# A hybrid attention block on one core: stick-breaking summed by parts, eight more gates by 7-product units, two branches moved beside the forgetting heads

## The chip, the cores and the metric

The kernel runs on one core of one Trainium2 chip. The metric is the time of the whole program on the device in microseconds (us), as the median of several runs; a profiled execution gives the trace. The engines that matter are TensorE (PE, with its weight loads as PEld), VectorE (DVE), ScalarE (ACT), GpSimd (POOL) and SyncE (SP); the last two mostly issue DMAs.

## What is computed

One decoder block over 1024 tokens of width 1024, in float32. The normalized input is projected into queries, keys and values of two kinds of attention with 8 heads of 64 each, queries of a memory attention with 4 heads of 128 over 256 memory tokens, 8 forget logits, and three gates of width 1024.

```python
z = einsum(q, k) * HD ** -0.5                       # stick-breaking, strictly causal
log_rem = where(strict, log_sigmoid(-z), 0.0)
after = cumsum(log_rem, reverse=True) - log_rem
w = where(strict, exp(log_sigmoid(z) + after), 0.0) # o_sb = w @ v
...
z = einsum(q, k) * HD ** -0.5 + F[t] - F[s]         # forgetting, F = cumsum(log f)
p = softmax(where(causal, z, NEG_INF))              # o_fox = p @ v
...
gates = sigmoid(gate_logit)
merged = gates[0] * (o_sb @ w_sb) + gates[1] * (o_fox @ w_fox) + gates[2] * (o_mem @ w_mem)
x = x + merged @ w_out
x = x + relu(rmsnorm(x) @ w_up) ** 2 @ w_down
```

## The kernel before

**Numbers.** A float32 operand is split into a high and a low part (`split`, L1027): ScalarE copies the high part, VectorE subtracts. A product takes three passes on TensorE (high-high, high-low, low-high). A matmul's free size is at most 512 columns, one PSUM bank.

**Order.** A planner written in Python (`Machine`, L186) runs generator processes at build time and emits the instructions of each engine in the order in which its own cost estimates let them begin. A process yields an `Op` on an engine, a `Get` of a buffer from a list of places, a `Sleep`, or an event. `spawn(gen, late)` gives a process a priority: the smaller the number, the earlier it is served among those that wait. Operations with `side=True` run only when no other operation of that engine is ready; all projections and branches are of this kind, so they fill what the attention heads leave of TensorE. Each engine executes its emitted list in order, and waits on semaphores for what it needs.

**Stages.**
1. Norms of the tokens and their transposes (`prologue`), then values of the forgetting heads, gates 8 and 9 and the memory's keys and values.
2. Six *units* (`unit_products`, L1365), the projections `sbk, sbq, mq, fxk, fxq, sbv` of 512 output columns each, by a scheme of 7 block products in place of 8 (`KINDS`). Sums of weight blocks are made by `unit_prep`, results of the 7 products are added up by `unit_evict` (L1439) and brought into their final form by `unit_final` (L1468), through 10 buffers `SN`. Results go to DRAM scratch. `PP`, `SC` and `PV` banks are lent to the units and given back in the last one: two each.
3. Attention (`second_part`, `load_pairs`, `units`): 4 pairs of stick-breaking heads, then 4 pairs of forgetting heads; each pair has 8 units of two query tiles of 128. A tile's scores are made in chunks of 512 columns in one of two `SC` banks.
   - `sb_tile` (L786): ScalarE makes 1 - beta (`rho`) and beta of a chunk; VectorE masks the diagonal, scans `rho` from the right into running products, and multiplies beta by them.
   - `fox_tile` (L824): VectorE masks the diagonal, finds each chunk's maximum and its negative; ScalarE exponentiates with that and sums; then the two chunks' maxima are merged and ScalarE scales the whole tile by factor over sum.
   - `unit` (L875): the weights are transposed on TensorE, split by ScalarE and VectorE, multiplied with the values' high and low halves (which stand side by side in 128 columns); ScalarE and VectorE add both halves of the output, and SP stores it.
   - `memory` (L559): 4 heads by 2 halves, each in `mem_attention`; starts once the last stick-breaking pair is over, so it runs beside the forgetting heads. It uses `RR` tiles (three, shared with `sb_tile`) and `HT` tiles (head operands; 12 + 7 + 4).
   - Filler for TensorE: the 22 other gates (`dense_gate`, `dense_T`), 2 halves of 8 blocks by 3 passes each. Gates 16 to 23 get their sigmoid at eviction, the others are stored as they are and get it when they are used.
4. When all gates are done the normalized input is freed (`all_h`, event `closed`) and `O` tiles open in its place. Then three branches follow, memory (`dense_branch(0)`), stick-breaking (`dense_branch(1)`), forgetting (`last_branch`). `operands` (L1563) and `bring` (L1550) fetch head outputs from DRAM into `RAW` tiles and split them. A branch multiplies with the gate on VectorE from `PP` banks, of which there are four once the heads are over (`more_banks`).
5. The output projection, the norm, and the MLP, by 7-product schemes.

Loads of head operands, values, memory and gate weights are issued from GpSimd's queue, which is in order; outputs, gates and branch operands go through SP's.

Of the kernel before, what the change touches and what calls it, by code (L numbers as in the profile page):

```python
# [21 lines left out]
P = 128  # L22
# [21 lines left out]
def tile_hybrid_block(  # L44
# [40 lines left out]
    C = Pool("c", st=32, st16=8, ss=4)  # L85
# [10 lines left out]
    def mmbank():  # L96
# [6 lines left out]
    above = C.p.tile([P, P + 1], F32, tag="above", name="above")  # L103
    nc.gpsimd.memset(above, 0.0)
    nc.gpsimd.affine_select(out=above, in_=above, pattern=[[-1, P + 1]], compare_op=ALU.is_ge,
                            fill=NEG, base=0, channel_multiplier=1)
    tri, strict = above[:, :P], above[:, 1:]
# [10 lines left out]
    o_scr = [dram.tile([512, S], F32, name=f"o_scr{b}", tag=f"o_scr{b}") for b in range(3)]  # L118
    gate_scr = dram.tile([3 * D, S], F32, name="gate_scr", tag="gate_scr")
# [4 lines left out]
    v_scr = {k: dram.tile([P, ST * 512], F32, name=f"v_{k}", tag=f"v_{k}") for k in ("sb0", "sb1", "fx0", "fx1")}  # L124
    m_scr = [dram.tile([P, 4, 512], F32, name=f"m_scr{c}", tag=f"m_scr{c}") for c in range(2)]
# [5 lines left out]
    def stat(n, dt=F32):  # L131
        return (C.t("st", [P, 8], dt) if n <= 8 else C.t("st16", [P, 16], dt))[:, :n]
# [204 lines left out]
    ES, OO, EL, RR, HT, PH, PL, OB, VV, BK = (Places([]) for _ in range(10))  # L337
# [127 lines left out]
    def small_loads():  # L465
# [9 lines left out]
        def scale():  # L475
            nc.vector.tensor_scalar(gq2, gq2, HD ** -0.5, None, ALU.mult)
            nc.vector.tensor_scalar(gmq, gmq, P ** -0.5, None, ALU.mult)
# [81 lines left out]
    def memory():  # L559
        yield pairs[3].over  # L560
# [33 lines left out]

    def mem_attention(h, half, kv, q):
# [8 lines left out]
        def scores_of(t2):  # L604
# [9 lines left out]
            def maxima():  # L614
                nc.vector.tensor_reduce(mx, sc.rearrange("p (t m) -> p t m", m=MEM), AX.X, ALU.max)
                nc.vector.tensor_scalar(mx, mx, -1.0, None, ALU.mult)
# [7 lines left out]
            yield Op("DVE", dve_time(512) + SMALL, maxima)  # L624
# [161 lines left out]
    def sb_tile(pair, b, i, beta):  # L786
# [4 lines left out]
        def chunk(ci, c, m, u):  # L791
# [6 lines left out]
            def sigmoids():  # L798
                nc.scalar.activation(rho[:, c:c + u], sc[:, :u], AF.Sigmoid, scale=-HD ** -0.5)  # L799
                nc.scalar.activation(beta[:, c:c + u], sc[:, :u], AF.Sigmoid, scale=HD ** -0.5)  # L800

            yield Op("PE", mm_time(m, m), scores)
            if c + u == n:
                dg = sc[:, u - P:u]
                yield Op("DVE", 0.22, lambda: nc.vector.tensor_tensor(dg, dg, strict, ALU.add))
# [6 lines left out]
        def scan():  # L812
            rev = rho[:, n - 1::-1] if n == D else rho[:, 0:n][:, ::-1]
            nc.vector.tensor_tensor_scan(out=rev, data0=rev, data1=zero.to_broadcast([P, n]),  # L814
                                         initial=1.0, op0=ALU.mult, op1=ALU.add)

        def weights():
            nc.vector.tensor_tensor(beta[:, 0:n - 1], beta[:, 0:n - 1], rho[:, 1:n], ALU.mult)

        yield Op("DVE", 0.1 + 0.00215 * n, scan, 0.14)  # L820
        yield Op("DVE", dve_time(n), weights)
        RR.put(rho)

    def fox_tile(pair, b, i, e):  # L824
# [5 lines left out]
        st = stat(16)  # L830
        mx, nx, l, f, t_, m = (st[:, c0:c0 + 2] for c0 in range(0, 12, 2))

        def chunk(ci, c, cols, u):
# [6 lines left out]
            def maxima():  # L840
                if c + u == n:
                    dg = sc[:, u - P:u]
                    nc.vector.tensor_tensor(dg, dg, tri, ALU.add)
                nc.vector.tensor_reduce(mx[:, ci:ci + 1], sc[:, :u], AX.X, ALU.max)  # L844
                nc.vector.tensor_scalar(nx[:, ci:ci + 1], mx[:, ci:ci + 1], -1.0, None, ALU.mult)
            yield Op("PE", mm_time(cols, cols), scores)
            yield Op("DVE", (0.22 if c + u == n else 0.0) + dve_time(u) + SMALL, maxima)
# [653 lines left out]
    def second_part():  # L1501
# [11 lines left out]
        for ev in proj_over:  # L1513
            yield ev
# [1064 lines left out]
```

## Time and profile before

| | |
|---|---|
| median of 3 runs | 1707.92 us (1707.22 to 1709.28) |
| profiled execution | 1706.93 us |
| its span, first to last instruction | 1705.1 us |
| matmuls | 9186 |
| VectorE busy | 1346.3 us (79%) |
| ScalarE busy | 886.8 us (52%) |
| bytes moved by DMA | 271.72 MB |

How to read the rows: `L1119 PE MATMUL pp<-hi,whi` is an instruction of line 1119 on TensorE that writes tile `pp` and reads `hi` and `whi`; then come shapes, a count, and, after a bar, busy microseconds and mean nanoseconds of one, and, after another, the idle time of that engine just before them and whom it waited for. In the view of one line, three numbers with slashes are the least, median and greatest duration in ns, and two times are the first and last start. Tables by stretch give busy microseconds of each engine with the number of instructions. In a row of waits, the numbers are microseconds in total, how often, and the longest. A DMA row ends with KB of one transfer and the median us from issue to landing.

### The profile page before, as it was taken

The numbers are of one execution on the slowest core, as the hardware profiler recorded it, in microseconds if no ns is written. First come the engines' busy times: TensorE is split into PE (matmuls) and PEld (weight loads), VectorE is DVE, ScalarE is ACT, GpSimd is POOL, SyncE is SP. The second block draws the span as 40 slices with busy tenths as digits, with TensorE's granted clock in tenths as the row PEclk, the third lists the DMA queues.
The fourth block names the chain that finished last, engine by engine and source line by source line (L and its number), as shares of the span: only waits on it lengthen the run. The fifth ranks groups of instructions, "written<-read, shape, count | busy, mean of one in ns | idle before, by whom it ended". The sixth has DMA issues, their size and how long they took to land.

```text
span 1705.1 us, 25350 instructions
## 1 busy us (share of the span) xinstructions
PE 1691.7 (99%) x9186; PEld 1442.8 (85%) x9186; DVE 1346.3 (79%) x2321; ACT 886.8 (52%) x1635; POOL 256.0 (15%) x441
## 2 busy tenths in 40 slices
PE   9999999999999999999999999999999999999998
PEld 9998899998888888888888887878888887888887
DVE  7977678868999888888656898987777776788775
ACT  6445555556676798889733446533233344332331
POOL 0000000043322233241000011021211120000000
PEclk9999999999999999999999999999999999999999
DMA  7545444576544453553375642144444484554532
GB/s 242 162 144 191 135 124 149 157 245 187 160 128 123 113 176 112 183 164 110 100 238 168 217 179 94 56 162 141 156 153 149 142 289 180 195 206 148 198 123 74
DMA packets 131406, 271.72 MB, mean 159 GB/s; under 512 B 15761, under 2 KB 43409, under 8 KB 131281
## 3 DMA queue, kind: packets, MB, share of 16 engines
q1 hardware_dynamic: 99600, 169.94, 29.2%
q0 software_dynamic: 31680, 100.17, 19.5%
q8 instruction: 72, 1.18, 0.3%
q14 instruction: 54, 0.43, 0.1%
HBM read 181.44 MB, written 88.60 MB: 158 GB/s over the span
## 4 chain that ended last, share of the span: by engine, by line
PE 83%; issue 7%; DVE 5%; DMA 2%; POOL 2%; ACT 1%; SPq 0%; POOLq 0%; DVEq 0%; ACTq 0%
PE pp L1119 21%; PE pp L2518 7%; PE pp L1405 7%; PE pp L1848 6%; PE sc L1405 5%; PE tr L904 4%; PE tr L2518 4%; PE sc L2518 4%; PE sc L1119 3%; PE sc L1848 3%; PE pv L2518 2%; PE pv L921 2%; PE pp L921 2%; PE pv L1405 2%; POOL s_scr L1865 2%
## 5 line engine op out<-in xcount | busy, mean ns | idle before, releaser
L1119 PE MATMUL pp<-hi,whi 128*128 128x512 f32 x368 | 147.6, 401 | 0.0
L1119 PE MATMUL pp<-hi,wlo 128*128 128x512 f32 x368 | 145.0, 394 | 0.0
L1119 PE MATMUL pp<-lo,whi 128*128 128x512 f32 x368 | 144.8, 393 | 0.0
L1030 DVE TENSOR_TENSOR wlo<-raw,whi 128x1024 fp32r<-128x1024 f32 (+1 forms) x82 | 100.0, 1221 | 38.9 <-ACT whi L1029 38.6
L2518 PE MATMUL pp<-h,sop 128*128 128x512 f32 x540 | 128.7, 395 | 1.4 <-DVE sop L1784 1.4
L2518 PEld LDWEIGHTS pp<-h,sop 128*128 128x128 f32 x540 | 101.1, 187 | 26.5 <-DVE sop L1784 1.8
L1848 PE MATMUL pp<-h,oh 128*128 128x512 f32 x384 | 120.9, 396 | 0.7 <-ACT cu L1934 0.6
L1029 ACT ACTIVATE whi<-raw 128x1024 fp32r<-128x1024 f32 (+1 forms) x82 | 86.8, 1059 | 52.4 <-PE pp L1405 18.7
L911 DVE TENSOR_TENSOR ptl<-tr,pth 128x512 fp32r<-128x512 f32 (+1 forms) x160 | 98.8, 627 | 11.0 <-ACT pth L909 10.6
L909 ACT ACTIVATE pth<-tr 128x512 fp32r<-128x512 f32 (+1 forms) x160 | 86.7, 558 | 28.5 <-PE tr L904 15.5
L814 DVE TENSOR_TENSOR_SCAN r<-r,sm 128x896 f32<-128x896 f32 (+4 forms) x64 | 85.5, 1345 | 3.5 <-ACT r L799 3.4
L2436 ACT ACTIVATE h<-t 128x2048 fp32r<-128x2048 f32 x16 | 30.7, 1919 | 110.4 <-DVE t L1784 97.9
L1848 PEld LDWEIGHTS pp<-h,oh 128*128 128x128 f32 x384 | 71.7, 187 | 19.2 <-ACT cu L1934 1.5
L1119 PEld LDWEIGHTS pp<-hi,wlo 128*128 128x128 f32 x368 | 69.1, 188 | 16.4
L1119 PEld LDWEIGHTS pp<-lo,whi 128*128 128x128 f32 x368 | 69.5, 189 | 10.3
L1119 PEld LDWEIGHTS pp<-hi,whi 128*128 128x128 f32 x368 | 69.4, 189 | 10.1
L1848 PE MATMUL pp<-h,ol 128*128 128x512 f32 x192 | 75.9, 396 | 0.0
L1841 ACT ACTIVATE oh<-raw 128x512 fp32r<-128x512 f32 x64 | 39.4, 625 | 61.7 <-DVE raw L1784 61.7
L2518 PE MATMUL sc<-h,sop 128*128 128x512 f32 x264 | 63.4, 395 | 0.0
L2518 PE MATMUL tr<-h,sop 128*128 128x512 f32 x264 | 63.4, 395 | 0.0
L1784 DVE TENSOR_TENSOR sop<-ur,sop 128x2048 fp32r<-128x2048 f32 x27 | 61.7, 2286 | 1.7 <-ACT sop L2447 1.7
L844 DVE TENSOR_REDUCE st<-sc 128x1 f32<-128x512 f32 (+2 forms) x96 | 53.3, 555 | 9.3 <-PE sc L838 7.1
(586 smaller groups left out, 5102.9 us busy)
## 6 DMA issues: line engine op xcount, KB each, us to landing
ur<-s_scr SPq DMA_DIRECT2D x26, 1024.0 KB
raw<-w_in POOLq DMA_DIRECT2D x42, 512.0 KB, 5.2
raw<-w_up SPq DMA_DIRECT2D x60, 256.0 KB
s_scr<-s POOLq DMA_DIRECT2D x60, 256.0 KB, 2.5
g<-w_down SPq DMA_DIRECT2D x14, 1024.0 KB
s_scr<-cu POOLq DMA_DIRECT2D x48, 256.0 KB, 2.9
gate_scr<-o SPq DMA_DIRECT2D x44, 256.0 KB
o<-gate_scr SPq DMA_DIRECT2D x32, 256.0 KB
```

What stands on the lines that cost most here:

```text
L814: nc.vector.tensor_tensor_scan(out=rev, data0=rev, data1=zero.to_broadcast([P, n]), initial=1.0, op0=ALU.mult, op1=ALU.add)
L904: nc.tensor.transpose(tr[:, jj * 256 + a * P:jj * 256 + (a + 1) * P], es[a][:, j * P:(j + 1) * P], ident)
L909: yield Op("ACT", act_time(512 - lo_c), lambda: nc.scalar.activation(ph[:, lo_c:], tr[:, lo_c:], AF.Copy))
L911: yield Op("DVE", dve_time(512 - lo_c), lambda: nc.vector.tensor_tensor(pl[:, lo_c:], tr[:, lo_c:], f32(ph[:, lo_c:]), ALU.subtract))
L921: nc.tensor.matmul(pv[0][:, c_:256], pair.v[:, j, b, :], p_[:, jj * 256 + c_:(jj + 1) * 256], start=(k == 0 and n_ == 0 and i == 0), stop= ...
L1029: yield Op("ACT", 0.03 + act_time(m), lambda: nc.scalar.activation(hi, raw, AF.Copy))
L1030: yield Op("DVE", dve_time(m), lambda: nc.vector.tensor_tensor(lo, raw, f32(hi), ALU.subtract))
L1119: nc.tensor.matmul(ps, a_, b_, start=(first and i == 0), stop=(last and i == n - 1))
L1405: nc.tensor.matmul(out_, a_, b_, start=(first and n == 0 and j == 0), stop=(last and n == 3 and j == len(todo) - 1), skip_group_check=True)
L1784: nc.vector.tensor_tensor(out_, a_, b_, op)
L1848: nc.tensor.matmul(ps, w[a_][:, k * P:(k + 1) * P], h[b_][k], start=(first and k == 0 and i == 0), stop=(last and k == 3 and i == 2), skip ...
L2518: nc.tensor.matmul(ps, a_[:, c, qs], b_[:, c, :], start=(kind in ("P1", "P2", "P7") and c == 0 and i == 0), stop=(kind in ("P2", "P4", "P3 ...
```

## The change

- **Stick-breaking by parts.** The scan now computes the reverse running sum of the weights, C[s] = rho[s] * C[s+1] + beta[s], and the output is the sum over s of C[s] * (v[s] - v[s-1]). The multiply after the scan goes. The differences of values are made by a new process, `value_steps`: the unit `sbv` stores plain values to DRAM, the process reads them twice, once shifted by a row, subtracts, and splits. The signs of queries are turned so that one mask with a positive fill serves both kinds of heads.
- **Gates in units.** Gates 16 to 23 become two more units `ga` and `gb` at the end of the six, with 14 gates left as filler. Gates 0 to 7 now get their sigmoid at eviction.
- **Forgetting heads.** Mask, extremum and negation are one instruction; the second chunk uses the merged maximum, so only the first chunk is rescaled, on VectorE; the division by the sums is done on the output. Both halves of the output are stored separately, and added and scaled when the last branch's operands are fetched.
- **Order.** Memory starts after the first stick-breaking pair. The memory branch's operands are fetched into `RR` tiles once memory is over; the stick-breaking branch's follow when the first four pairs are over; the last branch's are fetched pair by pair. The four tiles that were added to `HT` out of a weight buffer are kept as `spare` for one operand at a time. Branches may run before the heads are over, with two `PP` banks.

Core of the diff:

```diff
     def memory():
 

-        yield pairs[3].over
+        yield pairs[0].over
...
+    def sums_kept(h0):
+
+        cols = fn[:, 8 * h0:8 * h0 + 16]
+        yield Op("DVE", SMALL, lambda: nc.vector.reciprocal(cols, cols))
+        yield Op("SP", 0.4, lambda: nc.sync.dma_start(
+            l_scr[h0:h0 + 2, :].rearrange("h (i p) -> p (h i)", p=P), cols, allow_slow_non_contiguous=True), 4.0)
...
         def scan():
-            rev = rho[:, n - 1::-1] if n == D else rho[:, 0:n][:, ::-1]
-            nc.vector.tensor_tensor_scan(out=rev, data0=rev, data1=zero.to_broadcast([P, n]),
-                                         initial=1.0, op0=ALU.mult, op1=ALU.add)
-
-        def weights():
-            nc.vector.tensor_tensor(beta[:, 0:n - 1], beta[:, 0:n - 1], rho[:, 1:n], ALU.mult)
+            rho_, beta_ = (t[:, n - 1::-1] if n == D else t[:, 0:n][:, ::-1] for t in (rho, beta))
+            nc.vector.tensor_tensor_scan(out=beta_, data0=rho_, data1=beta_, initial=0.0, op0=ALU.mult, op1=ALU.add)
 
         yield Op("DVE", 0.1 + 0.00215 * n, scan, 0.14)
-        yield Op("DVE", dve_time(n), weights)
...
             def maxima():
                 if c + u == n:
-                    dg = sc[:, u - P:u]
-                    nc.vector.tensor_tensor(dg, dg, tri, ALU.add)
-                nc.vector.tensor_reduce(mx[:, ci:ci + 1], sc[:, :u], AX.X, ALU.max)
-                nc.vector.tensor_scalar(nx[:, ci:ci + 1], mx[:, ci:ci + 1], -1.0, None, ALU.mult)
+                    nc.vector.tensor_tensor_reduce(sc[:, :u], sc[:, :u], holder["later"][:, 512 - u:512], 1.0, -NEG,
+                                                   ALU.add, ALU.min, nx[:, ci:ci + 1])
+                else:
+                    nc.vector.tensor_reduce(nx[:, ci:ci + 1], sc[:, :u], AX.X, ALU.min)
...
+            bias = nx[:, 0:1]
+            if ci == 0:
+                machine.fire(first_max)
+            else:
+                yield first_max
+                bias = m
+                yield Op("DVE", SMALL, lambda: nc.vector.tensor_tensor(m, nx[:, 0:1], nx[:, 1:2], ALU.min))
...
-        def scaled():
-            for ci, (c, _, u) in enumerate(ch):
-                nc.scalar.activation(e[:, c:c + u], e[:, c:c + u], AF.Copy, scale=f[:, ci:ci + 1])
-        yield Op("DVE", SMALL * (4 if two else 1), scale)
-        yield Op("ACT", act_time(*[u for _, _, u in ch]) + 0.0002 * n, scaled)
+            yield Op("ACT", 0.22, lambda: nc.scalar.activation(f, nx[:, 0:1], AF.Exp, scale=-1.0, bias=m), table=AF.Exp)
+
+            def scaled():
+                nc.vector.tensor_scalar(e[:, :512], e[:, :512], f, None, ALU.mult)
+                nc.vector.scalar_tensor_tensor(total, l[:, 0:1], f, l[:, 1:2], ALU.mult, ALU.add)
+            yield Op("DVE", dve_time(512) + SMALL, scaled)
...
+        if pair.kind == "fox":
+            yield Op("ACT", act_time(256), lambda: nc.scalar.activation(ob, pv[0][:, :256], AF.Copy))
+            PV.put(pv[0])
+
+            def halves():
+                nc.sync.dma_start(scr[rows, cols], ob[:HD, :])
+                nc.sync.dma_start(low_scr[rows, cols], ob[HD:, :])
+            yield Op("SP", 0.2, halves, 3.0)
...
-    PROJ = ("sbk", "sbq", "mq", "fxk", "fxq", "sbv")
+    GATES = {"ga": 16, "gb": 20}
+    PROJ = ("sbk", "sbq", "mq", "fxk", "fxq", "sbv", *GATES)
...
+        elif u in GATES:
+            gt = yield Get(SN)
+            yield Op("ACT", act_time(512), lambda: nc.scalar.activation(gt, src, AF.Sigmoid), table=AF.Sigmoid)
...
+    def value_steps():
...
+        for c in range(2):
+            yield in_scr["sbv", c]
+            yield Sleep(1.0)
+            evs = []
+            for g in range(4):
+                a, b, *got = yield Get(SN, 4)
+
+                def issue():
+                    for r0, t in ((1 + g * 256, a), (g * 256, b)):
+                        nc.sync.dma_start(t.rearrange("p (i n) -> p i n", i=2),
+                                          vr_scr[r0:r0 + 256, c * 256:(c + 1) * 256].rearrange("(i p) n -> p i n", p=P))
+                yield from transfer(issue, P * 4096, 0.2)
+                yield Op("DVE", dve_time(512), lambda: nc.vector.tensor_tensor(a, a, b, ALU.subtract))
+                SN.put(b)
+                evs.append((yield from put_values(a, f"sb{c}", 2 * g, got)))
+                SN.put(a)
+            for ev in evs:
+                yield ev
+            machine.fire(stepped[c])
...
+    def fetched_o(bi, k):
+
+        raw_ = yield Get(RAW if bi == 1 else RR)
+        raw, rows = raw_[:, :S], slice(k * P, (k + 1) * P)
+        yield from transfer(lambda: nc.sync.dma_start(raw, o_scr[order[bi][1]][rows, :]), P * S * 4)
+        if bi == 2:
+            t = yield Get(RR)
+            yield from transfer(lambda: nc.sync.dma_start(t, low_scr[rows, :]), P * S * 4)
+            yield Op("DVE", dve_time(S), lambda: nc.vector.tensor_tensor(raw, raw, t, ALU.add))
...
+            yield from transfer(sums, P * S * 4, 0.2)
+            yield Op("DVE", dve_time(S), lambda: nc.vector.tensor_tensor(raw, raw, t, ALU.mult))
+            RR.put(t)
+        brought[bi, k] = raw, raw_
...
         yield mem_over
...
+        spare = [tuple(w_[:, i * 512:(i + 1) * 512] for w_ in holder["spare"]) for i in range(2)]
+        spawn(bring(0, ks[0], lambda: spare), -10.0)
+        for i in range(1, 4):
+            spawn(bring(0, ks[i], in_O(i), closed), -10.0)
+        yield closed
+        spawn(last_operands(in_O))
+        for pair in pairs[:4]:
+            yield pair.over
+        for i in range(4):
+            if i == 2:
+                spawn(bring(1, ks[i], lambda: spare, branches[0].done), -3.0)
+                continue
             t = yield Get(HT, 4)
+            spawn(bring(1, ks[i], lambda t=t: four(t)), 1.0)
+
+    def last_operands(in_O):
+        for i in range(4):
+            yield pairs[4 + i].over
+            ev = spawn(fetched_o(2, ks[i]), -5.0)
+            spawn(bring(2, ks[i], in_O(i), branches[0].done, fetched_=ev), 8.0)
+            if i < 2:
+                yield ev
...
+        RR.put(*(yield Get(EL, 4)))
         for _ in range(2):
             PP.put((yield Get(SC)))
```

More of the change, by code (lines that the diff above doesn't have):

```diff
@@ L946, in unit @@
             VV.put(pair.v_)
+            if pair.kind == "fox":
+                yield from sums_kept(2 * pair.p)
             machine.fire(pair.over)
@@ L1521, in second_part @@
         pair = yield Get(WP)
-        HT.put(*(w_[:, i * 512:(i + 1) * 512] for w_ in pair for i in range(2)))
+        holder["spare"] = pair
     def gate_put(n):
@@ L1632, in body @@
                     two = []
[L1633 removed]
+                    for half, n in ((0, 0), (0, 2), (1, 0), (1, 2)):
                         cols = slice(half * 512, half * 512 + 512)
@@ L1680, in may_gate @@
         return (PROJ[-1], "P4") in p_ops
-    gates = [dense_gate(n, may_gate) for n in (*range(16, 24), *range(0, 8), *range(10, 16))]
+    gates = [dense_gate(n, may_gate) for n in (*range(16, 24), *range(0, 8), *range(10, 16)) if n // 4 * 4 not in GATES.values()]
     h_tasks = [dense_values("fx0", C_FXV, None, first_gate), dense_values("fx1", C_FXV + 256, fn)]
```

157 lines of the change are left out of this document (73 added, 84 removed).

## The prediction

> **What bounds the kernel now.** I read the page's busy times first, then its slices, then the busy times by stage.
>
> ```profile
> span 1705.1 us, 25350 instructions
> PE 1691.7 (99%) x9186; PEld 1442.8 (85%) x9186; DVE 1346.3 (79%) x2321; ACT 886.8 (52%) x1635; POOL 256.0 (15%) x441
> ...
> PE   9999999999999999999999999999999999999998
> ```
>
> TensorE is busy for 99% of the span, and in every slice. That alone is not proof, since a matmul's record is longer than the step to the next matmul; so I look at the pace. In the table by stage below, the length is followed by TensorE's busy time with its matmuls in brackets, then weight loads, VectorE, ScalarE, GpSimd and the granted clock (1.00 throughout). The last row is the one wait of TensorE that begins in the stage of the heads, from the table of waits.
>
> ```profile
> 372.00:857.00 485.00, 484.03 (x2861) 420.47 (x2861) 416.47 (x980) 373.66 (x894) 146.39 (x259) 1.00 0.49 146
> 857.00:945.00 88.00, 87.95 (x379) 71.07 (x378) 53.52 (x74) 31.29 (x44) 6.02 (x8) 1.00 0.65 208
> 1500.00:1550.00 50.00, 50.00 (x216) 40.14 (x215) 37.78 (x33) 17.43 (x10) 0.54 (x1) 1.00 0.48 173
> ```
>
> ```profile
> PE sc L795 <- ACT es L800: 1.0, 1, 1.0
> ```
>
> 1500 to 1550 holds only matmuls of 512 columns: 216 in 50 us, so 0.2315 us each. The two branches after the heads, 857 to 945, run at 88/379 = 0.2322, the same pace. The attention stage (372 to 857) has smaller matmuls, which hide nothing: VectorE is busy 86% and ScalarE 77% there, and TensorE, with both attention and gate products to choose from, waits there once, for 1.0 us. So time is TensorE work, and a change is worth what it takes off TensorE, less the holes that it opens.
>
> **Removed: 48 matmuls.** The gate projections are the first three groups here, and the last row belongs to the branches.
>
> ```profile
> L1119 PE MATMUL pp<-hi,whi x368: 388/394/484, 80.7 to 849.1; 128*128 128x512 f32 x184
> L1119 PE MATMUL pp<-lo,whi x368: 389/393/400, 80.9 to 849.3; 128*128 128x512 f32 x184
> L1119 PE MATMUL pp<-hi,wlo x368: 388/393/402, 81.2 to 849.6; 128*128 128x512 f32 x184
> ...
> L1119 PE MATMUL pp<-h,whi x96: 389/393/401, 849.8 to 937.8; 128*128 128x512 f32 x96
> ```
>
> The first and last start in them bound the stages, as in these rows of the stick-breaking sigmoid and of the last transposes of the heads:
>
> ```profile
> L799 ACT ACTIVATE r<-sc x96: 272/580/655, 366.8 to 595.5; 128x512 f32<-128x512 f32 x48, 128x384 f32<-128x384 f32 x16, 128x128 f32<-128x128 f32 x16, 128x256 f32<-128x256 f32 x16
> L904 PE MATMUL tr<-ident,es x160: 270/272/329, 394.2 to 840.4; 128*128 128x128 f32 x160
> ```
>
> 3 x 368 = 1104 is 48 for each of 23 gates (one stands elsewhere). Eight gates are 384 matmuls. A 7-product unit is 7 products x 2 banks x 4 blocks x 3 passes = 168, also of 512 columns, so two units are 336. The difference is 48, and 48 x 0.2315 = **-11.1 us**. The Trainium skill, "TensorE: Matmul & The Clock Gate" (section on the 56 ns gap), gives 215.7 ns for such a matmul; by it the saving would be 10.4 us. The trace shows 231.5, and the trace decides.
>
> **Moved: when that work runs.** The two units (336 x 0.2315 = 78 us) stand ahead of attention, whose first sigmoid (366.8) goes to about 445. The filler beside attention is then 14 gates (14 x 48 x 0.2315 = 156 us) and two branches (192 matmuls each, 44 us), in place of 22 gates (244 us): 156 + 89 = 245. From first sigmoid to the branches' end TensorE had 938 - 367 = 571 us of work; it now has 571 - 244 + 156 = 483, to about 928. It stays full if attention ends early enough for the third branch's operands to be ready by then.
>
> **Attention gets cheaper off TensorE.** These are its rows from 372 to 857.
>
> ```profile
> L844 DVE TENSOR_REDUCE st<-sc 128x1 f32<-128x512 f32 (+2 forms) x96 | 53.3, 555 | 9.3 <-PE sc L838 7.1
> ...
> L818 DVE TENSOR_TENSOR e<-e,r 128x1023 f32<-128x1023 f32 (+3 forms) x31 | 31.1, 1006 | 0.0
> L843 DVE TENSOR_TENSOR sc<-sc,above 128x128 f32<-128x128 f32 x64 | 18.7, 292 | 6.8 <-PE sc L838 5.7 <-ACT pth L909 0.8
> L818 DVE TENSOR_TENSOR es<-es,r 128x127 f32<-128x127 f32 (+3 forms) x32 | 15.3, 478 | 0.2
> L845 DVE TENSOR_SCALAR st<-st 128x1 f32<-128x1 f32 x96 | 14.7, 154 | 3.3
> ...
> L636 DVE TENSOR_SCALAR r<-r,st 128x256 f32<-128x256 f32 x32 | 9.5, 359 | 0.3
> ```
>
> ```profile
> L871 ACT ACTIVATE e<-e,st 128x512 f32<-128x512 f32 x64 | 37.6, 639 | 2.7 <-DVE st L865 1.8 <-DVE st L856 0.6
> L871 ACT ACTIVATE es<-es,st 128x128 f32<-128x128 f32 (+3 forms) x32 | 17.7, 561 | 0.6 <-DVE st L867 0.5
> ```
>
> Stick-breaking loses its weights multiply (L818): 31.1 + 15.3 = 46 us of VectorE; the scan now carries the sum itself and is as long. A forgetting chunk's mask, maximum and negation (L843 to L845: 18.7 + 53.3 + 14.7 = 87 us) become one instruction. Masked and reduced in one pass over two streams, it is not in the trace: at least a reduce (0.555), at most a reduce plus a mask (0.847). I take the low end, since L843 touches only 128 columns: 53 us, so -34 (bounds -34 to -5). New are 32 scalings of 512 columns: L636 has 0.36 for 256, so each is 0.36 to 0.72, 12 to 23 us in all, and I take 18. The small sums of L862 to L867 and half of the output adds (L940) go too; I leave them uncounted. So VectorE's 416 us fall by 46 + 34 - 18 = 62 (bounds 46 + 5 - 23 = 28 and 68), and ScalarE loses L871, 37.6 + 17.7 = 55 of 374. If attention shrinks as VectorE's time does, it lasts 474 x 354/416 = 403 us instead of 474 (366.8 to 840.4), and at the worst bound 474 x 388/416 = 442. None of this shortens the sum; it is cover.
>
> **Costed at nothing, and by what.** (1) The values are stored, read back twice (once shifted by a row), subtracted and split: 8 groups of two loads, one subtraction and the split. Cover is the two units' 78 us.
>
> ```profile
> raw<-w_b POOLq DMA_DIRECT2D x10, 512.0 KB, 4.3
> ```
>
> ```profile
> POOL h L979 <- PE sc L838: 78.5, 10, 19.4
> ```
>
> With 4.3 us for a 512 KB load (the two of a group are 256 KB each), and a subtraction and a split of about 0.7 each, a group is some 6 us, and all eight are 48. Without that cover, the excess over 78 would delay the buffers into which gates leave, and TensorE would stop once its two product banks are full, 11 us later. (2) The mask is made on GpSimd ahead of the first head loads: gates cover it. (3) Memory's loads now stand in GpSimd's in-order queue before stick-breaking's. That queue already waits up to 19.4 us at a time for head buffers (L979), with the gates' weight loads behind it, and TensorE has no hole from it. (4) Forgetting output goes out as two DMAs in place of one, 32 more on SP's queue, plus a few for the sums; nothing on TensorE waits for them until the third branch, and its price is in rival B. (5) The gate sigmoids move to evictions of the same length.
>
> **The hand-overs, not at nothing.** The rows are an operand's split on ScalarE and VectorE, a weight's split, a branch's multiply, and the longest scan.
>
> ```profile
> L1029 ACT ACTIVATE h<-raw 128x512 fp32r<-128x512 f32 x7 | 4.2, 625 | 5.1 <-PE pp L1119 5.1
> L1030 DVE TENSOR_TENSOR h<-raw,h 128x512 fp32r<-128x512 f32 x6 | 4.0, 688 | 5.9 <-ACT h L1029 5.9
> L1030 DVE TENSOR_TENSOR wlo<-raw,whi 128x1024 fp32r<-128x1024 f32 x22 | 26.7, 1216 | 1.3 <-ACT whi L1029 1.2
> L1651 DVE TENSOR_TENSOR g<-pp,o 128x512 f32<-128x512 f32 x1 | 0.7, 692 | 0.5 <-PE pp L1119 0.5
> L814 DVE TENSOR_TENSOR_SCAN r<-r,sm 128x1024 f32<-128x1024 f32 x8 | 18.2, 2278 | 0.5 <-ACT r L799 0.5
> ```
>
> Branch 0's first operand is made early, the next three only when the gates' input memory is closed. The first half needs 0.625 + 0.688 and two semaphore steps, some 1.7 us, against 3 matmuls (0.7 us) in hand: up to 1 us. Branch 1's third operand is split only after branch 0's end: 1.7 against 6 matmuls (1.4). If attention still runs its matmuls fill both. Bounds 0 and 5 us (three operands in a row, no attention); I take 1.5, near the sum of the two. **Sum:** -11.1 + 1.5 = -9.6. On the profiled execution (1706.9, span 1705.1) that is 1697.3; its time is 1.0 under the median of 1707.9, so the median becomes **1698.3**.
>
> **Rivals.** *A, no gain: two banks.* Branches used to have four product banks, two of them the score banks given over after the last head. Beside heads they have two. A half's 12 matmuls last 2.8 us, and in that time the other bank must be drained by one multiply of about 0.69, queued behind attention's VectorE work (a weights split of 1.2, a long scan of over 2). If each of the 32 halves loses 0.3 us, 10 us go: 1708. Against it: whenever a branch waits, attention may use TensorE.
>
> *B, slower: attention ends too late.* Memory now runs beside stick-breaking. Both take row tiles, three in all. When memory is over, the first branch's operands are fetched into those same tiles and three of them stay there until the gates' input memory closes. If stick-breaking is not done by then, it stands still, and behind it the forgetting heads, while gates alone run. The price is the last pair's chain, bare: the sums stored (4.3), output rows, low rows and sums read one after the other (3 x 4.3, by the 512 KB load), an add and a multiply of 1024 columns (2 x 1.2, as L1030's), the split (1.3): 21 us. It begins to show when attention lasts over 928 - 21 - 445 = 462 us, and costs its whole 21 from 483 on, the filler's own end: -9.6 + 21 gives 1719, more if the standstill is longer. How near that is, these rows say (memory's transposes, a table load):
>
> ```profile
> L651 PE MATMUL tr<-ident,r x64: 270/272/328, 647.0 to 791.7; 128*128 128x128 f32 x64
> ```
>
> ```profile
> L848 ACT ACT_TABLE_LOAD x1 | 1.3, 1283 | 0.0
> ```
>
> For it: memory's transposes span 145 us, and three of the four stick-breaking pairs take 3/4 of 229 (366.8 to 595.5) = 172, so memory may well end first. Against it: beside each other both are slower, stick-breaking has less to do, and there are 462 - 403 = 59 us in hand. Exponentials beside sigmoids also reload tables: 16 groups, at most 32 loads of 1.283 = 41 us of ScalarE; kept 86% busy, as VectorE was, it would need (374 - 55 + 41)/0.86 = 419 us, still below 462. The Trainium skill, "ScalarE: Activation LUTs" (What ACT_TABLE_LOAD costs), puts a switch at 2.66 us with its drain, which would be 85 us and 470 in place of 419, past the point where B decides by 8 us, which would give 1706; the trace has the 1283 ns of the load, and no run here shows the drain.
>
> *C, more gain.* TensorE idles 1705.1 - 1691.7 = 13.4 us in all and 485.00 - 484.03 = 1.0 beside the heads, so little is left to save there. The short steps between transposes and products, which no row prices, may shrink with a lighter VectorE; I allow 4 us: 1694.
>
> **How the numbers follow.** My forecast 0.68 (1695 to 1703), A 0.14 (1703 to 1711), B 0.14 (1711 to 1735), C 0.04. The range takes the forecast, C's end and most of A: 1693 to 1710, leaving out B and a little. The measurement tells 0.2% (3.4 us) from no change. Faster than that, below 1704.5, are forecast, C and 0.04 of A: 0.76. Within it 0.10 of A and 0.01 of B: 0.11. Slower: 0.13.
>
> **What would show it.** Right: TensorE has 9186 - 48 = 9138 matmuls, busy in every slice; attention's first sigmoid near 445; the third branch begins near 928 with no wait on TensorE before it; L818 and L871 have no successors and VectorE's sum falls below 1346. A shows as branch matmuls waiting for a VectorE multiply, B as a hole ahead of the third branch that ends with the splits of its last operand, or a stretch in which only gates run; many table loads between memory's exponentials would show the switch. Wrong altogether is a matmul count that has not fallen, or holes in the two new units for lack of weights.

## The result and the profile after

The changed kernel takes **1725.8 us** (median, 1723.8 to 1727.3) against 1707.6 beside it (1705.6 to 1709.3): 1.0106 times as long, 95% interval 1.0089 to 1.0124. Forecast was 1698.3. The profiled execution took 1725.42 us. These are the lines of its page that answer to those shown of before, and its DMA packets:

```profile
span 1723.6 us, 25117 instructions
...
PE 1688.6 (98%) x9138; PEld 1439.5 (84%) x9138; DVE 1295.9 (75%) x2064; ACT 857.1 (50%) x1555; POOL 257.9 (15%) x441
...
PE   9999999999999999997998999999999999999999
...
PEclk9999999999999999998999999999999999999999
...
DMA packets 149966, 284.33 MB, mean 165 GB/s; under 512 B 25105, under 2 KB 60945, under 8 KB 149842
```

The matmuls fell by 48 as counted. Yet the row of TensorE, full in every slice before, has a 7 and an 8, near 800 us and near 925. So the work did not grow; holes came. Four stretches of the table by stage hold most of them (length, then busy time of TensorE, weight loads, VectorE, ScalarE and GpSimd with instructions, granted clock, DMA share, GB/s):

```profile
425.00:450.00 25.00, 20.97 (x83) 16.28 (x82) 8.09 (x12) 7.92 (x14) 12.31 (x23) 0.93 0.91 284
800.00:825.00 25.00, 15.86 (x92) 13.72 (x91) 12.42 (x29) 8.21 (x24) 6.22 (x12) 0.80 0.60 136
875.00:900.00 25.00, 21.36 (x112) 18.29 (x111) 17.29 (x41) 14.65 (x40) 0.76 (x1) 0.86 0.55 175
925.00:950.00 25.00, 21.42 (x82) 16.56 (x81) 13.76 (x19) 3.00 (x4) 1.50 (x2) 0.86 0.74 189
```

TensorE lacks 20.4 of 100 us here, VectorE is idle as well, and the granted clock, 1.00 everywhere before, drops with each hole. The table of waits says on whom TensorE waited (in all, how often, longest):

```profile
PE pp L919 <- DVE ptl L909: 9.6, 2, 9.1
PE sc L840 <- ACT e L858: 3.8, 2, 3.6
PE sc L1417 <- ACT sn L1456: 3.6, 1, 3.6
```

TensorE's long waits are for an operand that VectorE has to make (`ptl`), and for banks that ScalarE has to empty (`e` at L858, `sn` at L1456). The same table for VectorE, the rows of transfers alone:

```profile
DVE sn L1546 <- DMA sn<-vr_scr: 24.3, 6, 6.5
...
DVE r L1616 <- DMA r<-low_scr: 12.1, 3, 10.2
...
DVE o L1724 <- DMA o<-gate_scr: 8.5, 2, 8.1
```

How the second table makes the first is seen in the timeline of VectorE at the largest hole (start, length, engine, line, operation; in brackets the idle time ahead of it and what ended it), and in that of TensorE:

```profile
804.31 0.69 DVE L909 TENSOR_TENSOR ptl<-tr,pth 128x512 fp32r<-128x512 f32 x1 [0.60 <-ACT pth L907]
815.22 1.23 DVE L1616 TENSOR_TENSOR r<-r,r 128x1024 f32<-128x1024 f32 x1 [10.21 <-DMA r<-low_scr]
816.36 0.69 DVE L909 TENSOR_TENSOR ptl<-tr,pth 128x512 fp32r<-128x512 f32 x1
```

```profile
817.10 0.58 PE L919 MATMUL pp<-ptl,v 128*128 128x256 f32 x1 [9.14 <-DVE ptl L909]
...
817.90 1.05 PE L1129 MATMUL pv<-h,whi 128*128 128x512 f32 x2
818.76 0.63 PE L1129 MATMUL pv<-h,wlo 128*128 128x512 f32 x1
```

VectorE has reached the add of output rows and low rows (L1616), an operand of the last branch that nobody needs for over 100 us. Its low rows have not landed, and an engine that works in order does nothing else: the next instruction in its stream, the attention residue `ptl` (L909), comes 12.05 us after the one before it, and TensorE stands 9.14 us for it. After the hole two matmuls of 512 columns take 818.76 - 817.90 = 0.86 us, 0.43 each in place of the 0.2315 of before. The queue of SP shows what stands ahead of the low rows:

```profile
797.06 0.41 SPq L597 DMA_DIRECT2D l_scr<-fn  x1
800.48 0.46 SPq L1685 DMA_DIRECT2D o<-gate_scr  x1
800.99 0.43 SPq L1615 DMA_DIRECT2D r<-low_scr  x1
```

The load was issued at 800.99 and ended VectorE's wait at 815.22, 14.2 us later, where the planner allows about 4. Ahead of it stands the store of one pair's sums: `sums_kept` writes 128 partitions x 16 numbers, turned, hence 2048 pieces of 4 bytes. Such a store follows each of the four forgetting pairs (752.8, 797.1, 864.0 and 916.3 us).

The hole of 3.6 us that ends at 883.41 has the same form, through ScalarE. Its splits of an operand wait for rows (`raw`) issued at 866.88, behind the store of 863.98, and the exponential that would empty TensorE's score bank (L858) comes after them:

```profile
881.68 0.63 ACT L1039 ACTIVATE h<-raw 128x512 fp32r<-128x512 f32 x1 [4.87 <-DMA raw<-o_scr]
```

The first store opens no hole. The DMA engines slow down behind it too (the last two figures of this row are their busy share and GB/s), but neither VectorE nor ScalarE waits for a transfer then, and TensorE is busy throughout:

```profile
760.00:764.00 4.00, 4.00 (x29) 3.65 (x27) 2.46 (x7) 2.54 (x6) 2.26 (x5) 1.00 0.27 11
```

The first theory was therefore: these stores, and engines that work in order behind the loads that they delay.

### The profile page after: what moved, and what is told of

It is laid out like the page before. It is cut to its first block, busy times and chain, and to the rows that moved or that the text cites. A ratio compares the mean times of both kernels' runs of the same rounds, so it can differ in the third digit from the quotient of the medians.

```text
span 1723.6 us, 25117 instructions
## 1 busy us (share of the span) xinstructions
PE 1688.6 (98%) x9138; PEld 1439.5 (84%) x9138; DVE 1295.9 (75%) x2064; ACT 857.1 (50%) x1555; POOL 257.9 (15%) x441
## 2 busy tenths in 40 slices
DMA packets 149966, 284.33 MB, mean 165 GB/s; under 512 B 25105, under 2 KB 60945, under 8 KB 149842
## 4 chain that ended last, share of the span: by engine, by line
PE 67%; issue 14%; DMA 6%; DVE 5%; POOL 3%; ACT 1%; SPq 0%; POOLq 0%; DVEq 0%; ACTq 0%
PE pp L1129 10%; PE pp L1417 7%; PE pp L2592 7%; PE pv L1129 6%; PE sc L1417 5%; PE pp L919 4%; PE tr L2592 4%; PE sc L2592 4%; PE tr L902 3%; POOL s_scr L1939 3%; PE pv L2592 2%; DMA sn<-vr_scr 2%; PE pv L1417 2%; DMA o<-gate_scr 2%; PE pp L1922 1%
## 5 line engine op out<-in xcount | busy, mean ns | idle before, releaser
L1040 DVE TENSOR_TENSOR wlo<-raw,whi 128x1024 fp32r<-128x1024 f32 (+2 forms) x88 | 106.4, 1210 | 53.8 <-ACT whi L1039 53.4
L1039 ACT ACTIVATE whi<-raw 128x1024 fp32r<-128x1024 f32 (+2 forms) x88 | 92.1, 1048 | 74.0 <-PE pp L1417 25.0
L909 DVE TENSOR_TENSOR ptl<-tr,pth 128x512 fp32r<-128x512 f32 (+1 forms) x160 | 98.9, 629 | 27.6 <-ACT pth L907 27.1
L919 PE MATMUL pp<-ptl,v 128*128 128x256 f32 x320 | 79.3, 282 | 9.6 <-DVE ptl L909 9.6
L919 PE MATMUL pp<-pth,v 128*128 128x256 f32 x320 | 87.7, 297 | 0.0
L1334 POOL DMA_DIRECT2D raw<-w_in x28 | 21.2, 756 | 359.3 <-DVE wlo L1040 359.3
L919 PEld LDWEIGHTS pp<-ptl,v 128*128 128x128 f32 x320 | 61.4, 192 | 12.4 <-DVE ptl L909 10.1
L819 DVE TENSOR_TENSOR_SCAN e<-r,e 128x896 f32<-128x896 f32 (+3 forms) x32 | 60.3, 1886 | 11.7 <-ACT e L804 11.5
L919 PEld LDWEIGHTS pp<-pth,v 128*128 128x128 f32 x320 | 61.0, 191 | 2.3
L902 PE MATMUL tr<-ident,e 128*128 128x128 f32 x416 | 61.9, 273 | 0.5 <-DVE ptl L909 0.5
L2592 PEld LDWEIGHTS sc<-h,sop 128*128 128x128 f32 x264 | 49.6, 188 | 12.0
```

The costliest lines, as they stand in the source:

```text
L819: nc.vector.tensor_tensor_scan(out=beta_, data0=rho_, data1=beta_, initial=0.0, op0=ALU.mult, op1=ALU.add)
L902: nc.tensor.transpose(tr[:, jj * 256 + a * P:jj * 256 + (a + 1) * P], es[a][:, j * P:(j + 1) * P], ident)
L909: yield Op("DVE", dve_time(512 - lo_c), lambda: nc.vector.tensor_tensor(pl[:, lo_c:], tr[:, lo_c:], f32(ph[:, lo_c:]), ALU.subtract))
L919: nc.tensor.matmul(pv[0][:, c_:256], pair.v[:, j, b, :], p_[:, jj * 256 + c_:(jj + 1) * 256], start=(k == 0 and n_ == 0 and i == 0), stop= ...
L1039: yield Op("ACT", 0.03 + act_time(m), lambda: nc.scalar.activation(hi, raw, AF.Copy))
L1040: yield Op("DVE", dve_time(m), lambda: nc.vector.tensor_tensor(lo, raw, f32(hi), ALU.subtract))
```

## The experiments

**The store in 64-byte pieces.** One line differs; every engine's order stays. The sums land in another order in memory, so this version serves for its time alone:

```
-            l_scr[h0:h0 + 2, :].rearrange("h (i p) -> p (h i)", p=P), cols, allow_slow_non_contiguous=True), 4.0)
+            l_scr[h0:h0 + 2, :].rearrange("h (a c) -> (h a) c", c=16), cols), 4.0)
```

> The order of all instructions is that of the changed kernel; only the four stores of the sums differ: 128 pieces of 64 bytes instead of 2048 of 4 bytes (the sums land in another order in memory, so that output differs from the reference's). Theory (the 2048-piece store holds up the low rows and the gates that are queued behind it, and VectorE stands still behind the add that waits for them): the holes of TensorE at 808 (9.1 us), 879 (3.6) and 924 to 944 (some 5) go, with the slower steps after each: 18 to 24 us less, 1702 to 1708. Rival (the loads are late from traffic at large, or VectorE is late from its own work): less than 5 us, 1721 to 1726.

1703.1 us, 0.9975 of before (0.9965 to 0.9984): 22.7 us less than the changed kernel. Its packets:

```profile
DMA packets 142286, 284.33 MB, mean 167 GB/s; under 512 B 17425, under 2 KB 53265, under 8 KB 142162
```

7680 packets fewer, 4 x (2048 - 128) exactly. The Trainium skill, "DMA: Bandwidth & Descriptors" (Rules for kernel authors), says that a last dimension that is not contiguous becomes one descriptor per element; this count agrees. What the pieces did to the stretch around the load shows in the table by stage, first of the changed kernel, then of this one:

```profile
801.00:805.00 4.00, 4.00 (x30) 3.61 (x29) 3.40 (x11) 1.85 (x8) 2.10 (x4) 1.00 0.16 8
805.00:809.00 4.00, 2.96 (x17) 2.36 (x15) 0.00 (x1) 0.75 (x3) 0.00 (x0) 1.00 0.22 13
809.00:813.00 4.00, 0.00 (x0) 0.00 (x0) 0.00 (x0) 0.00 (x0) 0.00 (x0) 0.63 0.59 113
```

```profile
801.00:805.00 4.00, 4.00 (x29) 3.61 (x28) 2.62 (x10) 2.07 (x7) 1.77 (x4) 1.00 0.95 287
805.00:809.00 4.00, 2.40 (x14) 1.90 (x13) 2.10 (x5) 0.00 (x0) 0.00 (x0) 1.00 0.17 42
809.00:813.00 4.00, 4.00 (x23) 3.28 (x23) 3.16 (x11) 2.94 (x9) 2.05 (x4) 1.00 0.80 194
```

The last two columns tell it. With the 4-byte pieces the DMA engines are 16% and 22% busy over these eight microseconds and move 8 and 13 GB/s: they are not loaded but stalled, with loads waiting. In the trace's packet records the pieces themselves pass in some 2 us, at 800 to 802. What comes behind is slow: packets of 2 KB take up to 1.8 us instead of 0.08, the low rows start at 811, and GpSimd's head loads, issued at 801.46, move nothing before 813. With the 64-byte pieces the engines are 95% busy in the first four, and the low rows, issued at 799.72, end VectorE's wait at 806.9, after 7.2 us in place of 14.2. TensorE's 4.0 us of nothing in the third row are 4.0 us of work. (Its 2.40 in the second row is a hole of 1.6 us that stays; VectorE still waits 2.7 us for the low rows.)

**The sums turned on TensorE**, which is what the kernel should do instead:

```
...
+        tr = yield Get(TR)
+        yield Op("PE", 0.11, lambda: nc.tensor.transpose(tr[:16, :P], cols, ident))
+        ob = yield Get(OB)
+        yield Op("DVE", SMALL, lambda: nc.vector.tensor_copy(ob[:16, :P], tr[:16, :P]))
...
+            l_scr[h0:h0 + 2, :].rearrange("h (i p) -> (h i) p", p=P), ob[:16, :P]), 2.5)
```

> The sums are turned on TensorE (one 128x16 transpose a pair) and stored as 16 rows of 512 bytes; all of the output is computed. Theory: as with the 64-byte pieces, 1702 to 1708, less or more some 3 us for another order of the work. Rival: 1721 to 1726.

1700.8 us, 0.9959 (0.9945 to 0.9973): 6.8 below before and 25.0 below the changed kernel. The wait on the low rows falls from 12.1 us to 0.5. Between forecast and measurement lie 27.8 us (-9.6 against +18.2), and these are 25.0 of them, on a kernel that computes all of the output.

**The store on GpSimd's queue**, its pattern unchanged (`nc.gpsimd.dma_start` for `nc.sync.dma_start`):

> The 2048 pieces of 4 bytes are stored as in the changed kernel, but issued on GpSimd's queue instead of SP's. Theory (the store holds up what is behind it in SP's queue: gates, low rows): SP's loads land in some 5 us again and the holes at 808, 879 and 924 to 944 go, but the weight and head loads behind the store on GpSimd's queue are late by as much, some 13 us; the branches' weights have slack, so 1705 to 1718. Rival (the pieces clog the DMA engines, whichever queue they come from): 1722 or more.

1732.8 us, 1.0158 (1.0141 to 1.0175). The rival was right, and this part of the theory fell: it is not the place in SP's queue. VectorE's timeline has the same wait at the same add, and the view of the store's line gives what the store takes:

```profile
817.69 1.23 DVE L1616 TENSOR_TENSOR r<-r,r 128x1024 f32<-128x1024 f32 x1 [11.08 <-DMA r<-low_scr]
```

```profile
L597 POOL DMA_DIRECT2D l_scr<-fn x4: 1165/1202/1221, 750.5 to 919.1; - x4
...
DMA to landing us min/median/max: 12.8/12.9/13.0
```

12.9 us from issue to landing for 8 KB, with a spread of 0.2, and a load issued on another queue waits as long as one behind it. The Trainium skill, "DMA: Bandwidth & Descriptors" (Issuing engines are not separate DMA queues), says that transfers run on the same 16 engines whoever issues them; these two runs agree.

The page of this run shows one thing more:

```profile
DMA packets 141902, 284.33 MB, mean 165 GB/s; under 512 B 17041, under 2 KB 52881, under 8 KB 141778
```

Beside the changed kernel's 25105, 8064 small packets are gone, 4 x (2048 - 32): on this queue the records hold each store as 32 packets of 256 bytes. Yet the 4 KB packets behind the second store take 1.1 to 1.6 us (medians of each us from 803 to 810) in place of 0.16. So the slowing does not hang on packets of 4 bytes in the records; what both versions share is 2048 places of 4 bytes in memory to be written.

**Half the pieces**: eight of the 16 columns as before (1024 pieces), the other eight in 128 pieces of 32 bytes.

> The changed kernel, with half of each store in 4-byte pieces (1024) and half in 128 pieces of 32 bytes (these sums land in another order, so that output differs from the reference's). Theory (the price goes with the number of pieces, some 13 us for 2048): low rows land 3 to 4 us earlier than in the changed kernel, and TensorE gets back about half of the 23 us, 1711 to 1717. Rival (any store of this form costs a fixed time): 1722 or more. Second rival (the price has a threshold, since other work covers the first microseconds): 1708 or less.

1719.4 us, 1.0071 (1.0054 to 1.0088): 6.4 us less, a little outside what the theory gave, and neither rival. VectorE's wait at the add is 8.4 us in place of 10.2. So the price does not go with the number of pieces alone: 0, 1024 and 2048 of them give 1703.1, 1719.4 and 1725.8, and the first half costs 16.3 us, the second 6.4. (The half version issues two stores a pair in place of one; what that adds was not separated.)

**The add placed 10 us later** in the changed kernel (`yield Sleep(10.0)` ahead of it):

> The stores stay as in the changed kernel; the planner places the add of output rows and low rows 10 us after the low rows' planned arrival, so that VectorE has other work ahead of it. Theory (the late transfer alone stops nothing; what stops TensorE is that VectorE stands in order behind the add): VectorE's waits on the low rows fall from 12 us to under 4 and the hole of 9.1 us at 808 goes with its slow steps, 8 to 12 us less, 1714 to 1718; the waits for gates stay. Rival (TensorE lacks its operands because the transfers themselves are late): under 3 us less, 1723 or more.

1731.6 us, 1.0149 (1.0134 to 1.0164): a miss, with a time in the rival's range. The add's wait is gone, but TensorE has a hole of 10.0 us all the same, at 860 to 870, and VectorE's timeline names the culprit:

```profile
867.80 1.22 DVE L1623 TENSOR_TENSOR r<-r,r 128x1024 f32<-128x1024 f32 x1 [10.82 <-DMA r<-l_scr]
```

It is the multiply by the sums, the next load of the same chain. The mechanism (an in-order engine behind a late load) is borne out, the cure not: with four stores and three loads behind each, moving one consumer lets another take its place.

**The value steps later**: the planner puts each subtraction 6 us later, the loads stay.

> Only the planner changes: it places the subtraction of the value steps 6 us later, so that VectorE does other work while the loads are under way. Theory (VectorE waits in order for loads that land later than planned; its 24 us of waits on them give the hole of 3.6 us at 434): that hole and the slow steps after it go, 4 to 6 us less, 1720 to 1722, if the later value steps do not delay stick-breaking. Rival (the two units are held by buffers, not by the subtraction): 1725 or more, as the buffers come free later.

1730.8 us, 1.0137 (1.0122 to 1.0152): a miss as well, again with the rival's time. VectorE's waits on these loads fall from 24.3 us to 5.1, but each step's loads are issued only after the step ahead, and so the eighth's are now issued at 465 instead of 428, when attention has begun, and that one wait of 5.1 us there comes with a hole of 11.7.

**The value steps' loads issued one step ahead**, on top of the turned sums:

```
...
+            fetched_ = spawn(steps_in(c, 0))
             for g in range(4):
+                yield fetched_
+                if g < 3:
+                    fetched_ = spawn(steps_in(c, g + 1))
+                yield Sleep(3.0)
+                a, b = pairs_[c, g]
                 yield Op("DVE", dve_time(512), lambda: nc.vector.tensor_tensor(a, a, b, ALU.subtract))
...
```

> On top of the turned sums: each value step's loads are issued before the step ahead of it is computed, and its subtraction is placed 3 us later. Theory (the wait of 7 us of VectorE on the last of these loads gives the hole of 4.2 us at 437, and steps after it at half pace): hole and slow steps go, 5 to 6 us less than with the turned sums alone, 1695. Rival (the hole belongs to the buffers of the second unit, of which the steps now hold more): 1700 or more.

**1692.2 us**, 0.9918 (0.9903 to 0.9933), the fastest of all: 13.8 us below its before. Its page, and the four stretches again:

```profile
span 1690.4 us, 25127 instructions
...
PE 1680.2 (99%) x9142; PEld 1434.8 (85%) x9142; DVE 1295.3 (77%) x2068; ACT 857.9 (51%) x1555; POOL 256.7 (15%) x441
```

```profile
425.00:450.00 25.00, 25.00 (x110) 20.33 (x109) 7.63 (x9) 10.48 (x19) 13.21 (x25) 1.00 0.86 254
800.00:825.00 25.00, 25.00 (x152) 21.81 (x151) 18.88 (x50) 15.49 (x43) 8.91 (x16) 1.00 0.80 242
875.00:900.00 25.00, 24.69 (x133) 20.54 (x132) 21.76 (x38) 12.22 (x26) 2.26 (x3) 1.00 0.57 174
925.00:950.00 25.00, 25.00 (x109) 20.26 (x108) 18.37 (x25) 11.22 (x13) 0.00 (x0) 1.00 0.87 311
```

99.7 of 100 us, at full clock. VectorE no longer waits on these loads at all, and the last is issued at 414 instead of 428. The hole belonged to the loads, not to the second unit's buffers. (Each subtraction is also placed 3 us later here; the two were not tried apart.)

**The eight gates as dense products again** (`GATES = {}`), first in the changed kernel, then on top of the version of 1692.2:

> The eight gates go back to dense products (48 matmuls more, 9186); the sums by parts, memory and the branches stay as changed. Theory (the units save what their matmuls cost, and the loss is elsewhere): 11 us more, 1737, with holes of the same kind. Rival (the units bring the hole at 434 and starve attention of work beside it): under 1726.

> The version with turned sums and loads ahead, its eight gates back as dense products (9190 matmuls). Theory (the two units give 11.1 us by their matmuls and cover the value steps besides; bare, eight steps of at least 6 us less what gates can fill leave a hole of some 20 us ahead of the first values): 1692 + 11 + 20 = 1723, between 1712 and 1735. Rival (with loads that VectorE never waits for, dense gates cover the steps as well as the units do): 1692 + 11 = 1703.

1768.1 us, 1.0356 (1.034 to 1.0371), and 1750.7, 1.0257 (1.024 to 1.0274): both above what the theories gave, 42.3 and 58.5 us more than with the units, and far beyond the 11.1 of their matmuls. The longest waits of TensorE, of the first and of the second:

```profile
PE tr L902 <- DVE ptl L909: 42.1, 1, 42.1
PE pp L1129 <- ACT whi L1039: 13.0, 1, 13.0
```

```profile
PE tr L908 <- DVE ptl L915: 24.9, 1, 24.9
PE pp L1135 <- ACT whi L1045: 12.5, 1, 12.5
```

The first row of each is the value steps, bare: VectorE's in-order stream is held by them from about 380 us on, attention and gates with it, which loading ahead shortens but does not fill. The second row lies at the end, in the second kernel at 892 us: attention's last transposes there start at 852, so nothing fills a wait for a branch's weights. The units are worth their matmuls and, more than that, the 78 us of work that they put over the value steps: of the second kernel's 58.5 us the matmuls are 11.1 and these two holes 24.9 and 12.5; the other 10.0 were not split.

**Memory after the fourth stick-breaking pair**, as before the change (`pairs[3].over`), on top of the turned sums:

> On top of the turned sums: memory starts after the fourth stick-breaking pair, as before the change, instead of after the first. Theory (memory's place is neutral as long as attention ends in time; it takes no TensorE work away): 1699 to 1704. Rival (memory has to be early because it frees the input to the branches, which are TensorE's only work at the end): a hole ahead of the branches or beside the last forgetting heads, 1706 or more.

1730.2 us, 1.0139 (1.0124 to 1.0154), 29.4 more: the rival was right. The gate and branch products (L1135 here) between 800 and 870 us, in this kernel and in the version of 1692.2:

```profile
800.00:870.00 70.00, 13.71 (x51) 8.96 (x50) 0.90 0.52 159
```

```profile
800.00:870.00 70.00, 39.05 (x141) 25.18 (x141) 1.00 0.68 197
```

Memory's transposes end at 832 us instead of 694 as in the changed kernel, the branches' operands are fetched only after that, and the last forgetting heads run with hardly anything beside them.

**The stores added to the kernel before**, written to a place that nobody reads:

> The kernel before the change, with the four stores of 2048 pieces of 4 bytes added after each forgetting pair, to a place that nobody reads. Theory (a store costs TensorE time only where an in-order engine has a load to wait for behind it; before the change no load beside the heads feeds VectorE from SP's queue, and the branches' gates are read later): 0 to 6 us more, 1706 to 1713. Rival (the store itself takes 6 us a time from TensorE, through its weights and heads): 1725 or more.

1718.6 us, 1.0068 (1.0051 to 1.0085): 11.8 us more, between theory and rival. The loads that the theory overlooked are the branches' gates and operand rows. VectorE's longest wait on a transfer is for a gate, and TensorE's longest wait is for weights that ScalarE has to split:

```profile
DVE g L1657 <- DMA o<-gate_scr: 6.5, 1, 6.5
```

```profile
PE pp L1125 <- ACT whi L1035: 3.4, 1, 3.4
```

Those weights come late because ScalarE, in order, first stood 10.3 us for an operand's rows (`raw<-o_scr`), where its longest wait on such rows was 5.1 without the stores. So about half of the 22.7 to 25.0 us needs no new consumer. That the rest is what the change hung behind the stores is by elimination; no run shows it alone.

## Why the prediction was wrong

It forecast 9.6 us less; 18.2 more came. By the differences from the kernel before, run beside each: turning the sums takes 25.0 of it back (+18.2 to -6.8), loading the value steps ahead 7.0 more (to -13.8), and the remainder beats the forecast by 4.2: -9.6 + 25.0 + 7.0 - 4.2 = 18.2.

- **The step that failed** is the fourth of "Costed at nothing": "plus a few for the sums; nothing on TensorE waits for them until the third branch". The four stores were counted as four ordinary issues on SP's queue, though the form of their pieces stood in the change; rival B put 4.3 us on one, from the row of a 512 KB load. And "nothing on TensorE waits" follows the data only. The add and the multiply stand in VectorE's stream in the midst of attention, so that everything that VectorE makes next waits with them. Runs: 12.9 us for the store, 14.2 for a load behind it, 22.7 to 25.0 of the kernel's time for all four.
- **The value steps** were costed at 6 us a group, 48 in all under 78. From the loads of the first group (362.9) to those of the eighth (427.8) are 64.9 us, 9.3 a group, still under 78. The total was covered; it was again the wait in VectorE's stream, 24.3 us in six parts, that reached TensorE, for 3.6 us at 434. Load ahead shows the price: 8.6 us between the two medians, 7.0 beside their befores.
- **The 48 matmuls** are right by count (9138), and no run separates the 11.1 us alone; the two runs without units show that the cover was worth more than the saving.
- **Work moved**: the first sigmoid came at 451.4 (445 forecast) and at 444.8 without the hole at 434. In the version of 1692.2 the third branch begins here, near the 928 forecast:

```profile
L151 PE MATMUL sc<-h,wlo x28: 388/398/398, 927.3 to 971.2; 128*128 128x512 f32 x28
```

- **Attention cheaper off TensorE**: VectorE fell by 1346.3 - 1295.9 = 50.4 us (62 taken, bounds 28 to 68). The masked minimum was the mis-sized part. Beside the scaling it stands in the groups of the changed kernel between 440 and 930 us:

```profile
L845 DVE CUSTOM_DVE_ANT_0 sc<-sc,later 128x384 f32<-128x384 f32 (+1 forms) x64 | 31.5, 495 | 16.5 <-PE sc L841 14.6 <-issue 0.7 <-ACT es L858 0.6
...
L848 DVE TENSOR_REDUCE st<-sc 128x1 f32<-128x512 f32 x32 | 22.0, 687 | 7.3 <-PE sc L841 7.2
...
L869 DVE TENSOR_SCALAR e<-e,st 128x512 f32<-128x512 f32 x32 | 15.4, 481 | 4.7 <-ACT st L866 4.7
```

31.5 + 22.0 = 53.5 are the 53 forecast, but each masked minimum is followed by a read of its accumulator of 0.14 us, 9 more. The scaling took 15.4 for 18. ScalarE fell by 29.7 of the 55 in L871's rows; 15 table loads of 1.283 us from the first sigmoid to the branches' end, where before had 5, are 13 us of the difference.
- **Rivals.** A did not show: in the version of 1692.2 no wait of a branch's matmul on a multiply exceeds 0.3 us, and in the changed kernel the one of 2.4 us (at 932.97) stands behind a multiply that itself waited 8.1 us for its gate. B has the measured time in its range, 1711 to 1735, but by luck, since it named another mechanism: memory was over by 694 us with stick-breaking at its end, and no standstill came. Its premise that memory's place decides is true in reverse: later would have cost 29.4 us. C had 4 us of room; 1690.4 against 1705.1 less 11.1 is 3.6 better, its size.

What stays open: why transfers of both queues crawl for some ten microseconds behind a store whose own packets have passed. The same slowing behind 256-byte packets on GpSimd's queue speaks against the packets' size; whether the size of the places written, their number in one row of memory or where they lie makes it was not tried.

## What to carry to other kernels

An instruction that waits for a transfer is not off the critical path because its result is needed late: on an engine that works in order, what counts is who is queued behind it, and by when the transfer lands in the worst traffic. So look at the shape of each new transfer before its size, turn a small table on TensorE rather than in its store, and issue loads a step ahead; placing the consumer later without an earlier load only hands the wait to the next one. And a unit that saves matmuls may be worth more as cover: take it out alone and see.

## What the runs showed of the hardware

- 8 KB in pieces of 4 bytes: 12.9 us from issue to landing on GpSimd's queue, and for some ten microseconds transfers of both queues crawl; with the store on SP's queue the DMA engines were 16 to 22% busy at 8 to 13 GB/s. In 64-byte pieces of the same bytes no such stall shows.
- A hole of TensorE costs more than its length. After 9.1 us of it matmuls of 512 columns ran at 0.43 us each instead of 0.23. By the trace's clock records the granted clock of the changed kernel falls to 0.50 four times, with the holes of 3.60, 9.14, 3.64 and 2.40 us, and stays there for 3.41, 10.24, 6.83 and 6.83 us. The version without holes has 1.00 in all four stretches. The Trainium skill, "TensorE: Matmul & The Clock Gate" (Part 1), puts the clock's window at about 3.4 us and has the clock fall after at least one idle window. The lengths, one, three, two and two times 3.41 us, agree with such a window. The start does not: the clock fell 3.6, 2.1, 1.9 and 2.4 us after the last matmul had ended, and a hole of 2.40 us was enough. (The holes of the kernel before, up to 1.56 us, cost no clock.)
